# Moving the statistics and scaling of the gated branch into the gate pairs of a fused encoder layer

## The chip, the cores and the metric

The kernel runs on one core of one Trainium2 chip. The metric is the device time of one execution, in microseconds (us). The core's engines each run their own instruction stream in order and meet at semaphores: TensorE (PE, matrix products), VectorE (DVE, element-wise work and statistics), ScalarE (ACT, activations and copies), GpSimd (POOL, here a few element-wise operations and two short reciprocal-root steps) and SyncE (SP, which issues most of the loads).

## The reference

One layer of an encoder on x of 512 tokens by 1024 features, all in float32. The part around the change is the spatial gating branch (SGU):

```python
h = _rmsnorm(x, g_pre_mix)
proj = h @ w_in
q, k, v, g, u, sv, a_ret, a_sgu = jnp.split(proj, list(np.cumsum(IN_SPLITS)[:-1]), axis=-1)
y_ret = _retention_branch(q, k, v, g, ret_decay_logit, w_ret_o)
y_sgu = _sgu_branch(u, sv, sgu_ln_g, sgu_ln_b, w_spatial, b_spatial, w_sgu_o)
merged = jax.nn.sigmoid(a_ret) * y_ret + jax.nn.sigmoid(a_sgu) * y_sgu
x = x + _rmsnorm(merged @ w_out, g_post_mix)
...
def _sgu_branch(u, sv, sgu_ln_g, sgu_ln_b, w_spatial, b_spatial, w_sgu_o):
    u = jax.nn.gelu(u)
    sv = _layernorm(jax.nn.gelu(sv), sgu_ln_g, sgu_ln_b)
    svc = sv.reshape(B, S // CHUNK, CHUNK, SGU_GROUPS, SGU_GW)
    mixed = jnp.einsum('gpq,bnqgc->bnpgc', w_spatial, svc) + b_spatial.T[None, None, :, :, None]
    y = u * mixed.reshape(B, S, SGU_W)
    return y @ w_sgu_o
```

After it a second residual block follows: an RMS norm, an up projection to 2 x 2816, a convolution over three tokens, a gate and a down projection. The retention branch is a chunkwise recurrence over four heads, of which only the layer-normalized, gated result matters here: it is the input of w_ret_o.

## The kernel before

Products are taken in float32 accuracy from float32r halves: each weight block is split into a high part, which ACT copies (L95), and a low part, which DVE subtracts (L112), and three products are summed. Many products of the input with w_in run as a two-by-two Strassen (Winograd) scheme of seven smaller products; the weight forms it needs (T1 to T4, differences and sums of the weight blocks) are made on DVE or POOL (L194, L195, L197, L200) ahead of their splits. Raw weights come in by loads of 512 KB that SP issues (L165 for an ordinary block, L187 and L188 for the two halves of a Strassen pair) into four buffers named raw; a load is issued when the last split that reads the buffer's old content is done.

The stages follow each other on PE: q and k; the retention heads; v, g and sv; four *u pairs*; four *gate pairs* for a_ret, each with two column blocks of w_ret_o; four gate pairs for a_sgu, each with two column blocks of w_sgu_o, which read y; W_out; the feed-forward block.

A pair (class `Pair`) makes two 128-column strips of u or of a gate for all 512 tokens by seven products of twelve 256-column matmuls (L901): `part1` has the product with the first half of x (copied from its bank to c0 by ACT), `second` (the other half, added to c0 by DVE, L922), S1 and S2 (S2 goes on in the bank that ACT copied from, and is copied to c1). `part2` has S3, whose copy DVE subtracts from S1's bank (L940). `part3` has the last two: one goes on in the first bank, and S4 goes on in S1's bank, so S4 waits for L940. Then DVE scales (L949, L954) and ACT applies the function (L950, L955). In the first u pair, S1 and S2 are written ahead of `second`. In a gate pair of a_ret, `f_block` (eight rows of three 512-column matmuls, L286 to L288) stands before `part2`, and a second `f_block` has `part3` in its middle.

`sv_group` makes sv: its products, the finishing additions on DVE (L762), gelu on ACT (L756), a bn_stats on DVE (L757) behind each of the eight gelus, four bn_aggr (L785), and a reciprocal root on POOL (L445, L448). `sv_norm` (L793, eight instructions) subtracts the mean and scales; it is written behind `part2` of the first u pair. `mix(j)` is the spatial mixing of one 128-column strip j of eight: eight matmuls (L984) on sv, and on DVE an addition of the bias (L978), a scale (L992), the product with u (L1000) and the split of y. mix(2j) and mix(2j+1) are written behind gate pair j.

A scheduler orders the written instructions for each engine; `tc.issue_after(i)` adds that what is written inside it comes behind instruction i. Within an engine the order is then fixed.

Of the kernel before, what the change touches and what calls it, by code (L numbers as in the profile page):

```python
# [10 lines left out]
F32 = mybir.dt.float32  # L11
F32R = mybir.dt.float32r
AF = mybir.ActivationFunctionType
ALU = mybir.AluOpType
# [33 lines left out]
def tile_block(ctx: ExitStack, tc, xT, x, wall, par, cs, wsp, bsp, gpost, gffn, out):  # L48
# [11 lines left out]
    def blk(dt=F32, n="blk", shape=(P, S)):  # L60
        return sb.tile(list(shape), dt, tag="blk", bufs=NBLK, name=nm(n))
# [9 lines left out]
    def hi192(n, dt=F32R):  # L71
        pad("hi192")
        return sb.tile([P, S], dt, tag="hi192", bufs=5, name=nm(n))

    def lo64(n, dt=F32R):
        pad("lo64")
        return sb.tile([P, S], dt, tag="lo64", bufs=5, name=nm(n))
# [19 lines left out]
    def two(t):  # L97
        return t.rearrange("p (n c) -> p n c", n=2)
# [21 lines left out]
    i = 0  # L120
    while i < NW:
        pair = [(f, i) for f in FORMS]
        if i == SV0:
# [3 lines left out]
            i = U0  # L127
# [6 lines left out]
        elif i == UP0 + 2 * COUPLES[0][0]:  # L134
# [3 lines left out]
            i = UP0 + 2 * COUPLES[-1][1] + 2  # L138
# [10 lines left out]
    v = nc.vector  # L149
# [144 lines left out]
    T0, T1 = slice(0, 256), slice(256, 512)  # L294
# [156 lines left out]
    for t in range(NT):  # L451
        for n in range(2):
# [3 lines left out]
                out=xt, in_=xt, func=AF.Square, accum_out=ss[:, 4 * n + t : 4 * n + t + 1]  # L456
# [19 lines left out]
    for c in range(19, 1, -2):  # L476
        v.scalar_tensor_tensor(
            out=lc, in0=lc, scalar=1.0 / c, in1=lb, op0=ALU.add, op1=ALU.mult
        )
    v.scalar_tensor_tensor(out=lc, in0=lc, scalar=1.0, in1=la, op0=ALU.add, op1=ALU.mult)  # L480
    with behind():
        v.tensor_scalar(out=lg, in0=lgt, scalar1=0.0, scalar2=None, op0=ALU.min)
    v.scalar_tensor_tensor(
        out=lg, in0=lc, scalar=-2.0, in1=lg, op0=ALU.mult, op1=ALU.add
# [5 lines left out]
    for m in range(8):  # L490
        t = blk(n="qkraw")
# [6 lines left out]
    for m in range(8):  # L498
        t = blk(n="swap")
# [33 lines left out]
    for i, op in enumerate((ALU.max, ALU.min)):  # L533
        v.tensor_scalar(
            out=near[:, i * P : (i + 1) * P], in0=dist[:, P : 2 * P], scalar1=0.0, scalar2=None, op0=op
# [182 lines left out]
    svz = {}  # L718
    sst = const("sst", [P, NT, 2, 6])
    smv = const("smv", [P, NT, 2])  # L720
    srstd = const("srstd", [P, NT])

    def sv_group():

        held = {}

        def product(bank, act, first, last):
            for kp in range(2):
                wh, wl = w_get()
                for t in range(2):  # L730
                    c = slice(t * P, (t + 1) * P)
                    for kk in range(2):
                        k, f = 2 * kp + kk, slice(kk * S, (kk + 1) * S)
                        ah, al = act(k)
                        for i, (a_, w_) in enumerate(((ah, wh), (ah, wl), (al, wh))):
                            nc.tensor.matmul(
                                bank[t], a_[:, c], turns(w_[:, f]), start=first and k == i == 0,
                                stop=last and k == 3 and i == 2, skip_group_check=True,
                            )
                yield  # L740

        def x_(k0, t):
            return lambda k: (xh[k0 + k][:, t], xl[k0 + k][:, t])

        def s_(n):
            return lambda k: forms[n][k]

        def save(n, bank, t0, nh):
            held[n] = [blk(n="sv") for _ in range(2)]
            for t in range(2):  # L750
                svz[t0 + t, nh] = held[n][t]
                copy(held[n][t], bank[t])

        def gelu(t, nh, src):
            z = svz[t, nh]
            nc.scalar.activation(out=z, in_=src, func=AF.Gelu_apprx_tanh, scale=rstd[:, t : t + 1])  # L756
            v.bn_stats(out=sst[:, t, nh, :], in_=z)  # L757

        def finish(n, bank, t0, nh, sub):
            for t in range(2):  # L760
                a, b = (bank[t], held[n][t]) if sub != "held" else (held[n][t], bank[t])
                (v.tensor_sub if sub else v.tensor_add)(held[n][t], a, b)  # L762
                gelu(t0 + t, nh, held[n][t])

        b0 = [ps(), ps()]
        yield from product(b0, x_(0, T0), True, False)
        save("M1", b0, 0, 0)
        b2 = [ps(), ps()]
        yield from product(b2, s_("S1"), True, False)
        save("M5", b2, 2, 1)  # L770
        yield from product(b0, s_("S2"), False, False)
        save("U2", b0, 0, 1)
        for _ in zip(product(b2, s_("S4"), False, True), product(b0, s_("S3"), False, False)):
            yield
        finish("U2", b2, 0, 1, "bank")
        finish("M5", b0, 2, 1, "held")
        b1 = [ps(), ps()]
        yield from product(b1, x_(4, T0), True, True)
        finish("M1", b1, 0, 0, "")
        yield from product(b0, x_(4, T1), False, True)  # L780
        for t in range(2):
            svz[2 + t, 0] = blk(n="sv")
            gelu(2 + t, 0, b0[t])
        for t in range(NT):
            v.bn_aggr(out=smv[:, t, :], in_=sst[:, t].rearrange("p a b -> p (a b)"))  # L785
        rsqrt(srstd, smv[:, :, 1], 1.0, NT)
        yield

    def sv_norm():
        for t in range(NT):  # L790
            for q in range(2):
                z = svz[t, q]
                v.tensor_scalar(  # L793
                    out=z, in0=z, scalar1=smv[:, t, 0:1], scalar2=srstd[:, t : t + 1],
                    op0=ALU.subtract, op1=ALU.mult,
                )


    ogh, ogl = [], []
# [73 lines left out]
    def f_block(ah, al, n, between=None):  # L873

        wh, wl = w_get()
        o = ps()
        for k in range(n):
            if between and k == n // 2:
                between()
            c = slice(k * P, (k + 1) * P)  # L880
            mm3(o, wh[:, c], wl[:, c], turns(ah[k]), turns(al[k]), k == 0, k == n - 1)
        return o

    class Pair:
# [31 lines left out]
        def part1(self, apart=False):  # L916

            c0, c1 = self.t

            def second():  # L920
                o = self.product(1, self.x(4, T0), True)
                v.tensor_add(two(c0[:, T0]), o, two(c0[:, T0]))  # L922

            o = self.product(0, self.x(0, T0), True)
            copy(two(c0[:, T0]), o)
            if not apart:
                second()
            self.product(2, self.s("S1"), True)
            o = self.product(0, self.s("S2"), False)
            copy(two(c1[:, T0]), o)  # L930
            if apart:
                second()
            if self.scale is not None:
                v.tensor_mul(c0[:, T0], c0[:, T0], self.scale[:, T0])
# [27 lines left out]
    for j in range(KD // 2):  # L962
        p = Pair(AF.Gelu_apprx_tanh, lambda: U_HOMES.pop()(), None, rbc)
        with tc.issue_after(summed) if j == 0 else ExitStack():
            p.part1(j == 0)
        if late:
            late.part3()
        p.part2()
        late = p
        uT += p.t  # L970
        if j == 0:
            sv_norm()
    yh, yl = [], []

    def mix(j):
        gs = slice((j // 2) * P, (j // 2 + 1) * P)
        add = tmp("add", (P, P))
        v.scalar_tensor_tensor(  # L978
            out=add, in0=rws[:, gs], scalar=col(LNB + j), in1=bst[:, gs],
            op0=ALU.mult, op1=ALU.add,  # L980
        )
        o = ps()
        for t in range(NT):
            nc.tensor.matmul(  # L984
                o[:, t * P : (t + 1) * P],
                svz[t, j // 4][:, (j % 4) * P : (j % 4 + 1) * P],
                wst[:, gs],
                start=True,
                stop=True,
            )  # L990
        m = tmp("mix")
        v.scalar_tensor_tensor(  # L992
            out=m.rearrange("p (t q) -> p t q", t=NT),
            in0=o.rearrange("p (t q) -> p t q", t=NT),
            scalar=col(LNG + j),
            in1=add[:, None, :].to_broadcast([P, NT, P]),
            op0=ALU.mult,
            op1=ALU.add,
        )
        v.tensor_mul(uT[j], m, uT[j])  # L1000
        h_, l_ = blk(F32R, "yh"), blk(F32R, "yl")
        split(h_, l_, uT[j])
        yh.append(h_)
        yl.append(l_)


    def gated_pair(ah, al, late=None):

        p = Pair(AF.Sigmoid, lambda: tmp("sig"), None, rbc)
        with tc.issue_after(late.last.ins) if late else ExitStack():  # L1010
            p.part1()
        if late:
            with tc.issue_after(p.last.ins):
                late.part3()
        o = [f_block(ah, al, KD)]
        p.part2()
        o.append(f_block(ah, al, KD, p.part3))
        return zip(o, p.t)

    r = []  # L1020
    for j in range(KD // 2):
        for o, t in gated_pair(ogh, ogl, late if j == 0 else None):
            b = (lo64("r", F32) if j == 0 else hi192("r", F32) if j < 3 else blk(n="r"))
            v.tensor_mul(two(b), in_turn(o), two(t))
            r.append(b)
        mix(2 * j)
        mix(2 * j + 1)
    mh, ml = [], []
    for j in range(KD // 2):
        for i, (o, t) in enumerate(gated_pair(yh, yl)):  # L1030
# [589 lines left out]
```

## Time and profile before

| | us |
|---|---|
| median of 3 runs | 794.61 (794.57 to 794.67) |
| profiled execution | 795.35 |
| its span, first to last instruction | 793.5 |
| PE busy | 778.5 (98%) |
| DVE busy | 647.9 (82%) |
| ACT busy | 460.7 (58%) |
| POOL busy | 90.7 (11%) |

The mean granted clock of PE is 0.994. Rows of a timeline give the start in the span, the duration (a matmul's includes its way through the array, so durations overlap), the engine, the line and operation, what it writes and reads, and in brackets how long the engine stood idle before it and what ended that. "x4" means four such instructions in a row. Where a row stands for several, its time is theirs together.

### The profile page before, as it was taken

The numbers are of one execution on the slowest core, as the hardware profiler recorded it, in microseconds if no ns is written. First come the engines' busy times: TensorE is split into PE (matmuls) and PEld (weight loads), VectorE is DVE, ScalarE is ACT, GpSimd is POOL, SyncE is SP. The second block draws the span as 40 slices with busy tenths as digits, with TensorE's granted clock in tenths as the row PEclk, the third lists the DMA queues.
The fourth block names the chain that finished last, engine by engine and source line by source line (L and its number), as shares of the span: only waits on it lengthen the run. The fifth ranks groups of instructions, "written<-read, shape, count | busy, mean of one in ns | idle before, by whom it ended". The sixth has DMA issues, their size and how long they took to land.

```text
span 793.5 us, 13415 instructions
## 1 busy us (share of the span) xinstructions
PE 778.5 (98%) x5139; PEld 723.2 (91%) x5139; DVE 647.9 (82%) x1118; ACT 460.7 (58%) x840; POOL 90.7 (11%) x105
## 2 busy tenths in 40 slices
PE   9999999999899999999999999999999999999996
PEld 8888998988798999999998898999999998999996
DVE  7469987989997877777766659999999889876887
ACT  6546557675655544444445677667777578744442
POOL 0010010010003011132210210001111012200001
PEclk9999999999899999999999999999999999999999
DMA  8755224112233322323349111335555365733244
GB/s 290 270 147 187 80 81 159 53 58 89 80 107 134 106 100 87 107 97 110 109 169 339 67 55 67 114 113 139 139 141 147 114 182 123 169 113 108 101 165 159
DMA packets 35535, 102.68 MB, mean 129 GB/s; under 512 B 4304, under 2 KB 6224, under 8 KB 35472
## 3 DMA queue, kind: packets, MB, share of 16 engines
q1 hardware_dynamic: 29216, 89.91, 33.6%
q0 software_dynamic: 5392, 10.75, 6.4%
q10 hardware_dynamic: 864, 1.18, 0.4%
q8 instruction: 40, 0.66, 0.3%
q14 instruction: 23, 0.19, 0.1%
HBM read 89.24 MB, written 4.19 MB: 118 GB/s over the span
## 4 chain that ended last, share of the span: by engine, by line
PE 63%; DVE 16%; DMA 7%; ACT 6%; issue 5%; POOL 1%; SPq 1%; POOLq 0%; DVEq 0%; ACTq 0%
PE ps L901 22%; PE ps L287 9%; PE ps L286 9%; PE ps L288 9%; DMA raw<-wall 4%; PE ps L1314 3%; PE ps L629 2%; PE ps L630 2%; PE ps L628 2%; DVE dl L112 2%; DVE sl L112 1%; PE ps L1064 1%; PE ps L1063 1%; PE ps L1062 1%; ACT wh L95 1%
## 5 line engine op out<-in xcount | busy, mean ns | idle before, releaser
L112 DVE TENSOR_TENSOR wl<-raw,wh 128x1024 fp32r<-128x1024 f32 (+1 forms) x84 | 95.8, 1150 | 46.6 <-PE ps L901 15.7
L95 ACT ACTIVATE wf<-raw 128x512 fp32r<-128x512 f32 x140 | 83.9, 624 | 79.7 <-PE ps L287 29.2
L901 PE MATMUL ps<-sh,wf 128*128 128x256 f32 x640 | 118.7, 278 | 5.1 <-ACT u L95 3.5
L112 DVE TENSOR_TENSOR wf<-raw,wf 128x512 fp32r<-128x512 f32 x140 | 101.4, 739 | 15.2 <-ACT wf L95 14.9
L901 PEld LDWEIGHTS ps<-sh,wf 128*128 128x128 f32 x640 | 103.2, 194 | 6.0 <-ACT u L95 3.6
L95 ACT ACTIVATE wh<-raw 128x1024 fp32r<-128x1024 f32 (+2 forms) x88 | 84.7, 974 | 31.9 <-DMA raw<-wall 15.3
L287 PE MATMUL ps<-h2l,wh 128*128 128x512 f32 (+1 forms) x256 | 90.2, 354 | 0.3 <-DVE h2l L1135 0.3
L288 PE MATMUL ps<-h2h,wl 128*128 128x512 f32 (+1 forms) x256 | 90.1, 353 | 0.0
L286 PE MATMUL ps<-h2h,wh 128*128 128x512 f32 (+1 forms) x256 | 90.1, 354 | 0.0
L901 PE MATMUL ps<-sl,wf 128*128 128x256 f32 x320 | 88.7, 277 | 0.0
L901 PEld LDWEIGHTS ps<-sl,wf 128*128 128x128 f32 x320 | 62.1, 194 | 0.4
L1314 PE MATMUL ps<-dl,fh 128*128 128x256 f32 x216 | 59.7, 276 | 0.3 <-DVE dl L112 0.3
L1314 PE MATMUL ps<-dh,fh 128*128 128x256 f32 x216 | 59.5, 275 | 0.0
L1314 PE MATMUL ps<-dh,fl 128*128 128x256 f32 x216 | 59.4, 275 | 0.0
L95 ACT ACTIVATE dh<-raw 128x768 fp32r<-128x768 f32 (+1 forms) x36 | 33.6, 949 | 36.2 <-DVE raw L220 21.4
L901 PE MATMUL ps<-xh,wf 128*128 128x256 f32 x288 | 53.7, 279 | 0.0
L288 PEld LDWEIGHTS ps<-h2h,wl 128*128 128x128 f32 x256 | 48.5, 190 | 5.1
L287 PEld LDWEIGHTS ps<-h2l,wh 128*128 128x128 f32 x256 | 48.6, 190 | 5.0 <-DVE h2l L1135 0.5
L286 PEld LDWEIGHTS ps<-h2h,wh 128*128 128x128 f32 x256 | 48.4, 190 | 4.8 <-ACT h2h L1132 0.3
L630 PE MATMUL ps<-wh,xl 128*128 128x512 f32 x128 | 48.5, 379 | 0.0
L629 PE MATMUL ps<-wl,xh 128*128 128x512 f32 x128 | 48.5, 379 | 0.0
L628 PE MATMUL ps<-wh,xh 128*128 128x512 f32 x128 | 48.5, 380 | 0.0
(335 smaller groups left out, 2147.9 us busy)
## 6 DMA issues: line engine op xcount, KB each, us to landing
raw<-wall SPq DMA_DIRECT2D x144, 512.0 KB, 3.6
x<-x SPq DMA_DIRECT2D x24, 256.0 KB, 5.7
fl<-gp POOLq DMA_DIRECT2D x12, 256.0 KB, 3.8
swap<-qkraw SPq DMA_DIRECT2D x16, 128.0 KB, 2.3
x<-x POOLq DMA_DIRECT2D x8, 256.0 KB, 2.4
fl<-fs POOLq DMA_DIRECT2D x8, 256.0 KB, 4.0
xT<-xT SPq DMA_DIRECT2D x7, 256.0 KB, 5.2
xT<-xT POOLq DMA_DIRECT2D x4, 256.0 KB, 4.0
```

The lines of the kernel that those rows point to most:

```text
L95: return nc.scalar.activation(out=o, in_=i, func=AF.Copy)
L112: nc.vector.tensor_sub(lo, src, as32(hi))
L286: nc.tensor.matmul(o, ah, bh, start=start, stop=False, skip_group_check=skip)
L287: nc.tensor.matmul(o, ah, bl, start=False, stop=False, skip_group_check=skip)
L288: nc.tensor.matmul(o, al, bh, start=False, stop=stop, skip_group_check=skip)
L628: nc.tensor.matmul(acc[t], xh[k][:, c], turns(wh[:, f]), start=k == 0, stop=False)
L629: nc.tensor.matmul(acc[t], xh[k][:, c], turns(wl[:, f]), start=False, stop=False)
L630: part_end[0] = nc.tensor.matmul(acc[t], xl[k][:, c], turns(wh[:, f]), start=False, stop=k == KD - 1)
L901: self.last = nc.tensor.matmul(o, w_[:, c], a_, start=first and k == n == 0, stop=k == 3 and n == 2, skip_group_check=True,)
L1062: nc.tensor.matmul(o, ah, turns(bh), start=k == 0, stop=False)
L1063: nc.tensor.matmul(o, ah, turns(bl), start=False, stop=False)
L1314: nc.tensor.matmul(o, a_[:, c], turns(w_[:, f]), start=j == t == i == 0, stop=j == DP - 1 and i == 2 and n not in (M2, M3, M4), skip_group ...
```

## The change

The bn_stats leave the gelus of sv's stage. A new function, `sv_stats`, holds all eight, the four bn_aggr, the reciprocal root and the first half of the scaling, `sv_norm(0)`; it is written in gate pair 0 behind `part2`, and nothing of it comes ahead of the addition of that pair's `second` (`p.sum`). `sv_norm(q)` now scales one half of the columns, four instructions; `sv_norm(1)` is written at the same place of gate pair 1. The first gate pair has no mixing behind it, the second has mix(0) and mix(1), the third three, the fourth three. The homes of the tiles r change so that the strips of sv and u that live longer have theirs. No instruction is added or removed on any engine. Lines shift in the changed kernel: L757 is now L788, L762 L761, L785 L789, L793 L796, L901 L904, L922 L925, L940 L943, L949 L952, L954 L957.

```diff
--- before.py
+++ after.py
@@ -754,7 +754,6 @@
         def gelu(t, nh, src):
             z = svz[t, nh]
             nc.scalar.activation(out=z, in_=src, func=AF.Gelu_apprx_tanh, scale=rstd[:, t : t + 1])
-            v.bn_stats(out=sst[:, t, nh, :], in_=z)
 
         def finish(n, bank, t0, nh, sub):
             for t in range(2):
@@ -781,19 +780,23 @@
         for t in range(2):
             svz[2 + t, 0] = blk(n="sv")
             gelu(2 + t, 0, b0[t])
+        yield
+
+    def sv_stats():
         for t in range(NT):
+            for nh in range(2):
+                v.bn_stats(out=sst[:, t, nh, :], in_=svz[t, nh])
             v.bn_aggr(out=smv[:, t, :], in_=sst[:, t].rearrange("p a b -> p (a b)"))
         rsqrt(srstd, smv[:, :, 1], 1.0, NT)
-        yield
-
-    def sv_norm():
+        sv_norm(0)
+
+    def sv_norm(q):
         for t in range(NT):
-            for q in range(2):
-                z = svz[t, q]
-                v.tensor_scalar(
-                    out=z, in0=z, scalar1=smv[:, t, 0:1], scalar2=srstd[:, t : t + 1],
-                    op0=ALU.subtract, op1=ALU.mult,
-                )
+            z = svz[t, q]
+            v.tensor_scalar(
+                out=z, in0=z, scalar1=smv[:, t, 0:1], scalar2=srstd[:, t : t + 1],
+                op0=ALU.subtract, op1=ALU.mult,
+            )
 
 
     ogh, ogl = [], []
@@ -919,7 +922,7 @@
 
             def second():
                 o = self.product(1, self.x(4, T0), True)
-                v.tensor_add(two(c0[:, T0]), o, two(c0[:, T0]))
+                self.sum = v.tensor_add(two(c0[:, T0]), o, two(c0[:, T0])).ins
 
             o = self.product(0, self.x(0, T0), True)
             copy(two(c0[:, T0]), o)
@@ -968,8 +971,6 @@
         p.part2()
         late = p
         uT += p.t
-        if j == 0:
-            sv_norm()
     yh, yl = [], []
 
     def mix(j):
@@ -1004,7 +1005,7 @@
         yl.append(l_)
 
 
-    def gated_pair(ah, al, late=None):
+    def gated_pair(ah, al, late=None, extra=None):
 
         p = Pair(AF.Sigmoid, lambda: tmp("sig"), None, rbc)
         with tc.issue_after(late.last.ins) if late else ExitStack():
@@ -1014,17 +1015,20 @@
                 late.part3()
         o = [f_block(ah, al, KD)]
         p.part2()
+        if extra:
+            with tc.issue_after(p.sum):
+                extra()
         o.append(f_block(ah, al, KD, p.part3))
         return zip(o, p.t)
 
     r = []
     for j in range(KD // 2):
-        for o, t in gated_pair(ogh, ogl, late if j == 0 else None):
-            b = (lo64("r", F32) if j == 0 else hi192("r", F32) if j < 3 else blk(n="r"))
+        for o, t in gated_pair(ogh, ogl, late if j == 0 else None, {0: sv_stats, 1: lambda: sv_norm(1)}.get(j)):
+            b = (lo64("r", F32) if j == 0 else blk(n="r") if j == 1 else hi192("r", F32))
             v.tensor_mul(two(b), in_turn(o), two(t))
             r.append(b)
-        mix(2 * j)
-        mix(2 * j + 1)
+        for i in ((), (0, 1), (2, 3, 4), (5, 6, 7))[j]:
+            mix(i)
     mh, ml = [], []
     for j in range(KD // 2):
         for i, (o, t) in enumerate(gated_pair(yh, yl)):
```

The scheduler's order moves in three places. On ACT, at the first u pair, these rows stand before; `sv` are the gelus, `rws` a row sum of the spatial weights, `wf` splits of weights, and the two `u` are the copies of the first bank (S2 waits for the first):

```order
L756 ACTIVATE sv_1794<-sv_1794,rstd 128x512
L756 ACTIVATE sv_1795<-sv_1795,rstd 128x512
L756 ACTIVATE sv_2206<-ps_1731,rstd 128x512
L756 ACTIVATE sv_2209<-ps_1732,rstd 128x512
L95 ACTIVATE rws_1909<-ps_2219 128x512
L95 ACTIVATE wf_2169<-raw_2104 128x512
L95 ACTIVATE wf_2184<-raw_2098 128x512
L95 ACTIVATE wf_2191<-raw_2187 128x512
L95 ACTIVATE wf_2230<-raw_2188 128x512
L95 ACTIVATE u_2225<-ps_2227 128x256
L95 ACTIVATE u_2226<-ps_2227 128x256
```

and these now:

```order
L756 ACTIVATE sv_1794<-sv_1794,rstd 128x512
L95 ACTIVATE wf_2159<-raw_2093 128x512
L756 ACTIVATE sv_1795<-sv_1795,rstd 128x512
L95 ACTIVATE wf_2163<-raw_2100 128x512
L95 ACTIVATE wf_2178<-raw_2094 128x512
L756 ACTIVATE sv_2200<-ps_1731,rstd 128x512
L95 ACTIVATE wf_2185<-raw_2181 128x512
L756 ACTIVATE sv_2202<-ps_1732,rstd 128x512
L95 ACTIVATE rws_1909<-ps_2204 128x512
L95 ACTIVATE wf_2215<-raw_2182 128x512
L95 ACTIVATE u_2210<-ps_2212 128x256
```

The first gelu pair no longer stand together, three weight splits stand between the gelus, and the split of the newest load (`wf_2230`, now `wf_2215`) still stands just ahead of the first copy; between the copies there are now splits. On PE, three of the twelve matmuls of `second` stood between S1 and S2 of this u pair before; now the twelve of each product stand together, p0, S1, S2, `second`.

On DVE, in the same stretch, the statistics stand between the finishing additions and the splits before:

```order
L762 TENSOR_TENSOR sv_1794<-ps_2095,sv_1794 128x512
L762 TENSOR_TENSOR sv_1795<-ps_2096,sv_1795 128x512
L112 TENSOR_TENSOR wf_2165<-raw_2097,wf_2165 128x512
L757 BN_STATS sst<-sv_1794 128x6
L757 BN_STATS sst<-sv_1795 128x6
L200 TENSOR_TENSOR raw_2104<-raw_2104,raw_2098 128x512
L757 BN_STATS sst<-sv_2206 128x6
L757 BN_STATS sst<-sv_2209 128x6
L112 TENSOR_TENSOR wf_2169<-raw_2104,wf_2169 128x512
L112 TENSOR_TENSOR wf_2184<-raw_2098,wf_2184 128x512
L112 TENSOR_TENSOR wf_2191<-raw_2187,wf_2191 128x512
```

and now:

```order
L761 TENSOR_TENSOR sv_1794<-ps_2091,sv_1794 128x512
L200 TENSOR_TENSOR raw_2100<-raw_2100,raw_2094 128x512
L112 TENSOR_TENSOR wf_2140<-raw_2094,wf_2140 128x512
L761 TENSOR_TENSOR sv_1795<-ps_2092,sv_1795 128x512
L112 TENSOR_TENSOR wf_2159<-raw_2093,wf_2159 128x512
L112 TENSOR_TENSOR wf_2163<-raw_2100,wf_2163 128x512
L112 TENSOR_TENSOR wf_2178<-raw_2094,wf_2178 128x512
L194 TENSOR_TENSOR raw_2231<-raw_2181 128x512
L112 TENSOR_TENSOR wf_2185<-raw_2181,wf_2185 128x512
```

The bn_stats are gone, and the addition L200 and a split of `raw_2094` stand between the two finishing additions, ahead of the split of `raw_2093`; the latter was `raw_2097` before, and its buffer takes the next load.

On DVE in gate pair 0, before, behind the additions of the u pair before it; L940 with `sig_2721<-ps_2724` is the difference for which S4 of this gate pair waits:

```order
L112 TENSOR_TENSOR wl_2757<-raw_2754,wh_2756 128x1024
L194 TENSOR_TENSOR raw_2825<-raw_2772 128x512
L949 TENSOR_TENSOR u_2594<-ps_2596,rbc_574 128x256
L112 TENSOR_TENSOR wf_2776<-raw_2772,wf_2776 128x512
L195 TENSOR_TENSOR raw_2772<-raw_2772,raw_2773 128x512
L952 TENSOR_TENSOR u_2595<-ps_2598,u_2595 128x256
L112 TENSOR_TENSOR wf_2822<-raw_2773,wf_2822 128x512
L954 TENSOR_TENSOR u_2595<-u_2595,rbc_574 128x512
L978 SCALAR_TENSOR_TENSOR add_2945<-rws_1909,part,bst_2223 128x128
L112 TENSOR_TENSOR wf_2829<-raw_2825,wf_2829 128x512
L112 TENSOR_TENSOR wf_2857<-raw_2825,wf_2857 128x512
L940 TENSOR_TENSOR sig_2721<-ps_2724,sig_2721 128x256
```

and now, from the second bn_aggr on:

```order
L789 BN_AGGR smv<-sst 128x2
L788 BN_STATS sst<-sv_1910 128x6
L788 BN_STATS sst<-sv_2202 128x6
L789 BN_AGGR smv<-sst 128x2
L788 BN_STATS sst<-sv_1911 128x6
L789 BN_AGGR smv<-sst 128x2
L112 TENSOR_TENSOR wf_2806<-raw_2802,wf_2806 128x512
L112 TENSOR_TENSOR wf_2834<-raw_2802,wf_2834 128x512
L796 TENSOR_SCALAR sv_1794<-sv_1794,smv,srstd 128x512
L943 TENSOR_TENSOR sig_2698<-ps_2701,sig_2698 128x256
L796 TENSOR_SCALAR sv_1795<-sv_1795,smv,srstd 128x512
L796 TENSOR_SCALAR sv_2200<-sv_2200,smv,srstd 128x512
```

Ahead of that difference, now L943 with `sig_2698<-ps_2701`, stand all eight bn_stats, four bn_aggr and the first of the norms, which waits for POOL; three more norms stand behind it.

## The prediction

> **What bounds the kernel now.** The page's busy line (us, share of the span, instructions) is read first: TensorE (PE) is the bound.
>
> ```profile
> PE 778.5 (98%) x5139; PEld 723.2 (91%) x5139; DVE 647.9 (82%) x1118; ACT 460.7 (58%) x840; POOL 90.7 (11%) x105
> ```
>
> So only what makes PE idle, or slows its clock, can change the time. PE's waits (second view: waited-for line, us in total, times, longest) name two that matter, one of 3.5 us and one of 1.6 us.
>
> ```profile
> PE ps L901 <- ACT u L95: 3.5, 1, 3.5
> PE ps L901 <- ACT sig L95: 1.6, 1, 1.6
> PE ps L388 <- PEq L1610: 0.8, 1, 0.8
> ```
>
> The third view, PE's timeline, places them. The first row is the last matmul of S1 before `second` of the first u pair; the third is its S2 product, waiting for ACT's copy of the first u bank; the fourth is S2 of gate pair 0.
>
> ```profile
> 203.85 0.28 PE L901 MATMUL ps<-sh,wf 128*128 128x256 f32 x1
> 203.97 0.28 PE L901 MATMUL ps<-xh,wf 128*128 128x256 f32 x1
> ...
> 204.19 0.28 PE L901 MATMUL ps<-xh,wf 128*128 128x256 f32 x1
> 207.92 0.58 PE L901 MATMUL ps<-sh,wf 128*128 128x256 f32 x1 [3.46 <-ACT u L95]
> ...
> 248.22 0.38 PE L901 MATMUL ps<-sh,wf 128*128 128x256 f32 x1 [1.65 <-ACT sig L95]
> ```
>
> Matmuls start 0.11 us apart, so the first stall delays issue by 207.92 - 204.30 = 3.62 us, the second by 1.65 + 0.28 - 0.11 = 1.82 us. The first costs more than its length. The stretches (length, PE, PEld, DVE, ACT, POOL busy, granted clock, DMA share, GB/s), cut where the clock can step:
>
> ```profile
> 203.32:206.73 3.41, 1.14 (x11) 0.95 (x9) 3.41 (x7) 3.40 (x7) 0.00 (x0) 0.96 0.46 154
> 206.73:210.15 3.42, 2.23 (x10) 2.23 (x11) 2.90 (x9) 1.03 (x3) 1.49 (x2) 0.50 0.43 149
> 210.15:213.56 3.41, 3.41 (x19) 3.41 (x18) 2.99 (x6) 2.05 (x4) 0.38 (x1) 0.54 0.04 10
> 244.28:247.69 3.41, 2.30 (x21) 2.10 (x19) 3.41 (x7) 2.39 (x6) 1.27 (x1) 1.00 0.02 4
> 220.00:240.00 20.00, 20.00 (x181) 20.00 (x181) 20.00 (x40) 12.80 (x26) 0.72 (x1) 1.00 0.30 98
> ```
>
> A stretch with PE 33% busy (1.14 of 3.41) is followed by two at half clock; one with 67% (2.30 of 3.41) is not. From 207.92 to 213.56 PE did at half clock what full clock does in about half of it: 5.64 x 0.48 = 2.7 us lost. The two stalls together cost 3.62 + 2.7 + 1.82 = 8.1 us.
>
> Why the first wait ends so late is read from the chain of waits (start, us, what) and from DVE's and ACT's timelines.
>
> ```profile
> 202.76 0.61 DVE wf L112
> ...
> 203.39 3.49 DMA raw<-wall
> ...
> 206.97 0.63 ACT wf L95
> 207.60 0.28 ACT u L95
> ...
> 207.92 14.09 PE ps L901 x101
> ```
>
> ```profile
> 191.32 0.68 DVE L757 BATCH_NORM_STATS2 sst<-sv 128x6 f32<-128x512 f32 x1
> ...
> 197.89 0.68 DVE L757 BATCH_NORM_STATS2 sst<-sv 128x6 f32<-128x512 f32 x1
> ...
> 203.28 1.28 DVE L757 BATCH_NORM_STATS2 sst<-sv 128x6 f32<-128x512 f32 x2
> 204.48 0.67 DVE L200 TENSOR_TENSOR raw<-raw,raw 128x512 f32<-128x512 f32 x1
> ...
> 208.06 0.42 DVE L785 BATCH_NORM_AGGREGATE smv<-sst 128x2 f32<-128x12 f32 x4
> ...
> 210.57 0.55 DVE L793 TENSOR_SCALAR sv<-sv,smv,srstd 128x512 f32<-128x512 f32 x1 [0.93 <-POOL srstd L448]
> ...
> 218.55 2.83 DVE L793 TENSOR_SCALAR sv<-sv,smv,srstd 128x512 f32<-128x512 f32 x6
> ```
>
> ```profile
> 202.20 1.33 ACT L756 ACTIVATE sv<-sv,rstd 128x512 f32<-128x512 f32 x2 [1.99 <-DVE sv L762]
> 203.44 1.25 ACT L756 ACTIVATE sv<-ps,rstd 128x512 f32<-128x512 f32 x2
> 204.58 0.59 ACT L95 ACTIVATE rws<-ps 128x512 f32<-128x512 f32 x1
> 205.19 2.41 ACT L95 ACTIVATE wf<-raw 128x512 fp32r<-128x512 f32 x4
> ```
>
> DVE, busy without a break, splits a weight form late (202.76); only that frees the raw buffer for the next load (203.39, landed 206.88); ACT has the split of that load queued ahead of the u copy. DVE's pitch is 0.60 us for a 512-column operation (two bn_stats in 1.28, the next row 1.20 later), 0.47 for a norm (six in 2.83), 0.34 for 256 columns, 0.10 for a bn_aggr.
>
> **The change, part by part.** *The first stall.* Eight bn_stats leave sv's stage. Four of them (191.32 to 197.89) stood ahead of the split at 202.76; the L200 addition, behind it before, now stands ahead of it. The split moves from 202.76 to 202.76 - 4 x 0.60 + 0.60 = 200.96, the load's issue to 201.6, its landing (3.49 later) to 205.1. ACT is then free too: from about 201.0 the order gives it three gelus (0.62 each, from the rows above), rws and three splits (0.55 each), to 205.1. Its split of the load (0.63) and the copy (0.28) end at 206.0; PE starts S2 at 206.1. Its S1 ends at 203.97 as before, and `second` now stands behind S2, so PE idles 2.15 us where it idled 3.62.
>
> *The clock behind it.* In 203.32 to 206.73 PE would be busy 0.81 us (to 204.13) and 0.61 (from 206.1): 42%, between the 33% that lowered the clock and the 67% that didn't. It is nearer to 33%, so I take a drop to half; but the next stretch would be full of matmuls, so only one is cold, 3.41 x 0.48 = 1.64 us instead of 2.7. Ends: 0 and 2.7. [...]
>
> *The second stall.* The wait for the sig copy is a queue behind DVE:
>
> ```profile
> 243.38 0.69 DVE L112 TENSOR_TENSOR wf<-raw,wf 128x512 fp32r<-128x512 f32 x1 [1.50 <-ACT wf L95]
> ...
> 246.56 0.68 DVE L954 TENSOR_TENSOR u<-u,rbc 128x512 f32<-128x512 f32 x1
> 247.16 0.41 DVE L940 TENSOR_TENSOR u<-ps,u 128x256 f32<-128x256 f32 x1
> ```
>
> ```profile
> 247.27 0.63 ACT L955 ACTIVATE u<-u 128x512 f32<-128x512 f32 x1 [0.54 <-DVE u L954]
> 247.81 0.37 ACT L95 ACTIVATE sig<-ps 128x256 f32<-128x256 f32 x1
> ```
>
> Between 190 and this place DVE loses 8 x 0.60 + 0.42 + 8 x 0.47 + 0.93 (the wait for POOL) = 9.9 us, while PE comes 2.5 to 4.2 us earlier. Walked with these pitches, DVE's L954 ends at P + 0.9 (P: start of gate pair 0 on PE, 242.39 before, about 239.8 after), the sig copy at P + 2.6; S2 needs it at P + 4.0. The stall goes: 1.82 us. Its cover is 1.4 us.
>
> *The new wait in gate pair 0.* Now DVE does there 8 bn_stats, 4 bn_aggr, the POOL round trip and a norm, all ahead of the difference (L943 after, L940 before) that frees the bank for PE's S4 product at P + 18.4. Before, that difference ran right behind the splits. What starts the sequence is a pair of loads:
>
> ```profile
> 238.57 8.42 SPq L165 DMA_DIRECT2D raw<-wall  x2
> 248.20 0.33 SPq L187 DMA_DIRECT2D raw<-wall  x1
> 248.80 0.33 SPq L188 DMA_DIRECT2D raw<-wall  x1
> ```
>
> ```profile
> 254.54 0.69 DVE L194 TENSOR_TENSOR raw<-raw 128x512 f32<-128x512 f32 x1 [2.00 <-DMA raw<-wall]
> ```
>
> By the walk they go out at P + 1.9 and P + 2.9. Loads take 3.5 us alone (203.39) but 6.3 us where three follow closely (248.20 to 254.54). After the landing DVE needs: L194 0.60, a 1024-column split 1.13, L195 0.60, L952 and L955 0.67, two splits and L957 1.8, six bn_stats 3.6, aggregates 0.4, POOL's trip 2.1 (from the end of the aggregates at 208.48 to the norm at 210.57; it hides two splits), the norm 0.47, L943 0.34: 11.7 us. So L943 ends at P + 1.9 + 6.3 + 11.7 = P + 19.9, and S4 waits 1.6 us; with 3.5 us it ends 1.3 us early and nothing waits. The order again sends three loads close together, so I take 1.6; ends 0 and 1.6.
>
> *The rest.* sv_norm(1) is four norms (1.9 us) in gate pair 1, where by the same walk S4's difference has about 3 us to spare. Six of the eight mixes move one pair later.
>
> ```profile
> L984 PE MATMUL ps<-wst,sv x64: 273/275/275, 266.7 to 333.0; 128*128 128x128 f32 x64
> ```
>
> Each is eight matmuls, about 0.9 us that PE spends either way, and on DVE three 512-column and one 128-column operation, about 2.1 us; what stands behind them on DVE is the second f_block's split, needed some 8 us later. Three mixes now end the last gate pair instead of two; the products that read y reach its last rows over 2.5 us after they are written. Cost nothing; that cover gone, the third mix would show as up to 2.1 us. POOL's two rsqrt rows move behind one L197, the r tiles' homes cost nothing, and SP's queue keeps its order.
>
> *Sum.* Before 8.1; after 2.15 + 1.64 + 1.6 = 5.4: 2.7 us faster. Against the profiled execution (795.35 us, span 793.5 and 1.85 around it; 0.74 above the median) that is 792.6; against the median 794.61 it is 791.9.
>
> **The rivals.** *No clock drop* (42% busy is enough): 2.15 + 1.6 = 3.75 left, 790.2; without the new wait 788.6. For it: no row shows how much a stretch must hold. Against it: 42% is nearer the row that dropped. [...]
>
> *About the same: the first load is slow.* If the load of 201.6 takes 6.3 us like those of 248.20, it lands at 207.9, PE starts at 208.9: 4.9 us idle, then 213.56 - 208.9 = 4.7 us cold, 2.2 lost; with 1.6 that is 8.7 against 8.1, 795.2. For it: DMA share was 0.46 there. Against it: the same load took 3.49 in the same place.
>
> *Slower: DVE is still behind when the statistics come.* DVE is busy 20.00 of 20.00 us from 220 to 240. If it reaches gate pair 0 as late against PE as before (L940 at P + 4.8, by my walk P + 1.3), everything behind shifts 3.5 us: S4 waits 5.1 us, long enough for a cold clock (two stretches, about 2.5), and the sig wait stays (1.8): 2.15 + 1.64 + 5.1 + 2.5 + 1.8 = 13.2, 5.1 us slower, 799.7. It decides from about 2.5 us behind my walk, where the S4 wait passes 4 us and brings a cold stretch. Against it: 9.9 us of work are gone and DVE idled 1.50 us at 243.38 even before.
>
> **Chances.** 0.2% is 1.6 us, about what a measurement of this kernel tells from no change. Forecast (one cold stretch) 0.42, its own range 790.2 to 793.2 (the new wait 0 to 1.6, and 1.3 for the walk's error); no drop 0.26; about the same 0.15; slower 0.17. Faster 0.68, same 0.15, slower 0.17. From 788.6 (no drop, no new wait) to 795.6 all but the slower case and a small tail lie inside.
>
> **What would show it.** Right: the u wait about 2 us, one half-clock stretch from 206.73, no sig wait, a PE wait of up to 1.6 us on DVE L943 near 258, no PE wait at the start of the second gates. Wrong: a u wait of 3 us or more, no or two cold stretches, or an S4 wait above 3 us with a cold stretch behind it.

## The result

The changed kernel takes 794.66 us (median of 20 runs, 792.79 to 797.39), the kernel before 794.69 us (20 runs, 793.33 to 797.09). The ratio is 1.0001, with a 95% interval of 0.9991 to 1.0011: the change moves the time by nothing that can be measured. The profiled execution of the changed kernel has a span of 794.4 us, the one of before 793.5.

Under that equal sum much has moved. PE's waits in the profile after (line waited for, us in total, times, longest):

```profile
PE ps L904 <- DVE sig L943: 3.3, 1, 3.3
PE ps L904 <- ACT u L95: 2.6, 2, 1.9
PE ps L388 <- PEq L1614: 0.8, 1, 0.8
```

And where they stand in PE's timeline: the first u pair, the last u pair (233.47) and S4 of gate pair 0 (261.09). Ahead of the two long waits stands the last matmul before them.

```profile
203.58 0.28 PE L904 MATMUL ps<-sh,wf 128*128 128x256 f32 x1
205.76 0.38 PE L904 MATMUL ps<-sh,wf 128*128 128x256 f32 x1 [1.91 <-ACT u L95]
...
233.47 0.38 PE L904 MATMUL ps<-sh,wf 128*128 128x256 f32 x1 [0.64 <-ACT u L95]
...
257.54 0.28 PE L904 MATMUL ps<-xh,wf 128*128 128x256 f32 x1
261.09 0.58 PE L904 MATMUL ps<-sh,wf 128*128 128x256 f32 x1 [3.27 <-DVE sig L943]
```

The first wait has shrunk, the wait for the sig copy is gone, and a wait for L943 has come. The stretches of the changed kernel's profile (length, PE, PEld, DVE, ACT, POOL busy, granted clock, DMA share, GB/s), cut where its clock steps:

```profile
201.82:205.24 3.42, 2.04 (x19) 1.84 (x17) 2.92 (x5) 3.26 (x7) 0.00 (x0) 1.00 0.71 216
205.24:208.65 3.41, 2.88 (x25) 2.89 (x26) 3.38 (x7) 2.53 (x6) 0.00 (x0) 1.00 0.26 96
256.44:259.85 3.41, 1.37 (x13) 1.18 (x11) 2.44 (x5) 0.00 (x0) 2.56 (x3) 1.00 0.00 0
259.85:263.26 3.41, 2.17 (x10) 2.18 (x11) 3.41 (x6) 0.00 (x0) 0.56 (x1) 0.50 0.00 0
263.26:266.68 3.42, 3.42 (x11) 2.88 (x11) 2.32 (x5) 2.54 (x4) 0.00 (x0) 0.50 0.48 153
```

In these two profiles the half-clock time has not gone: it has moved from behind the first u wait to behind the wait for L943, and there it is as long (two stretches) as it was before.

Taking the same matmul (by its number among the 5139) in the two traces, the changed kernel's start minus that of before is a running account (from 270 to 335 us PE's order differs between the two, so no row is taken there):

| place | after minus before, us | step |
|---|---|---|
| ahead of the first u wait | -0.3 | |
| behind it and behind the half clock of before | -4.4 | 4.1 won: a shorter wait, no half clock |
| behind the wait at 233 | -3.5 | 0.9 lost |
| behind the sig copy's place | -5.2 | 1.7 won |
| S4 of gate pair 0 starts | -1.7 | 3.4 lost: the wait for L943 |
| behind the half clock there | +1.1 | 2.8 lost |
| first products of the second half (515) | +0.9 | |
| last matmul | +0.6 | |

So 5.8 us were won, and 7.1 lost, of it 6.2 at one place. From there on the two run side by side; nothing is paid for the later mixing. This is an account of one execution of each kernel, and these two differ by 0.9 us where the medians don't differ.

Before, the difference came at 261.48 and PE at 262.80, so S4 didn't wait:

```profile
261.48 0.42 DVE L940 TENSOR_TENSOR sig<-ps,sig 128x256 f32<-128x256 f32 x1
```

```profile
262.80 0.28 PE L901 MATMUL ps<-sh,wf 128*128 128x256 f32 x1
```

Now PE is there at 257.65. Why L943 comes only at 260.62, in the changed kernel's DVE timeline:

```profile
241.49 0.41 DVE L943 TENSOR_TENSOR u<-ps,u 128x256 f32<-128x256 f32 x1
...
247.11 0.69 DVE L194 TENSOR_TENSOR raw<-raw 128x512 f32<-128x512 f32 x1 [1.16 <-DMA raw<-wall]
247.72 1.22 DVE L112 TENSOR_TENSOR wl<-raw,wh 128x1024 fp32r<-128x1024 f32 x1
248.85 1.77 DVE L195 TENSOR_TENSOR raw<-raw,raw 128x512 f32<-128x512 f32 x1
250.54 0.41 DVE L952 TENSOR_TENSOR u<-ps,rbc 128x256 f32<-128x256 f32 x1
...
256.91 0.21 DVE L789 BATCH_NORM_AGGREGATE smv<-sst 128x2 f32<-128x12 f32 x1
257.04 1.24 DVE L112 TENSOR_TENSOR wf<-raw,wf 128x512 fp32r<-128x512 f32 x2
259.21 1.49 DVE L796 TENSOR_SCALAR sv<-sv,smv,srstd 128x512 f32<-128x512 f32 x1 [0.93 <-POOL srstd L448]
260.62 0.41 DVE L943 TENSOR_TENSOR sig<-ps,sig 128x256 f32<-128x256 f32 x1
```

and in its POOL timeline:

```profile
248.69 1.38 POOL L197 TENSOR_TENSOR raw<-raw,raw 128x512 f32<-128x512 f32 x1 [8.81 <-DMA raw<-wall]
257.21 0.52 POOL L445 TENSOR_SCALAR rs<-smv 128x4 f32<-128x4 f32 x1 [7.14 <-DVE smv L789]
257.81 1.36 POOL L448 TENSOR_TENSOR srstd<-rs,nhalf 128x4 f32<-128x4 f32 x1
259.16 1.25 POOL L200 TENSOR_TENSOR raw<-raw,raw 128x512 f32<-128x512 f32 x1
```

From the landing (247.11) to the end of L943 (261.03) DVE takes 13.9 us, where the prediction had 11.7. The difference is in two rows: L195 occupies DVE 1.69 us to the next row instead of 0.60, and the norm 1.41 instead of 0.47. Both begin inside an addition of POOL (248.69 to 250.07, 259.16 to 260.41), and they end 0.55 and 0.29 us after it.

### The profile page after: what moved, and what is told of

Same layout as the page of the kernel before. It is cut to its first block, busy times and chain, and to the rows that moved or that the text cites. A ratio compares the mean times of both kernels' runs of the same rounds, so it can differ in the third digit from the quotient of the medians.

```text
span 794.4 us, 13407 instructions
## 1 busy us (share of the span) xinstructions
PE 778.2 (98%) x5139; PEld 723.0 (91%) x5139; DVE 652.3 (82%) x1118; ACT 461.5 (58%) x840; POOL 86.9 (11%) x105
## 4 chain that ended last, share of the span: by engine, by line
PE 78%; DVE 13%; DMA 3%; issue 2%; ACT 2%; POOL 1%; POOLq 0%; DVEq 0%; SPq 0%; ACTq 0%
PE ps L904 18%; PE ps L286 11%; PE ps L287 11%; PE ps L288 11%; PE ps L1318 10%; PE ps L628 3%; PE ps L629 3%; PE ps L630 3%; DMA raw<-wall 3%; DVE wf L112 2%; DVE sl L112 2%; PE ps L1334 2%; PE ps L1068 1%; PE ps L1067 1%; PE ps L1066 1%
## 5 line engine op out<-in xcount | busy, mean ns | idle before, releaser
L904 PE MATMUL ps<-sh,wf 128*128 128x256 f32 x640 | 118.7, 278 | 5.8 <-DVE sig L943 3.3
L904 PEld LDWEIGHTS ps<-sh,wf 128*128 128x128 f32 x640 | 102.8, 194 | 7.0 <-DVE sig L943 3.5
L904 PE MATMUL ps<-sl,wf 128*128 128x256 f32 x320 | 88.6, 277 | 0.0
L904 PEld LDWEIGHTS ps<-sl,wf 128*128 128x128 f32 x320 | 62.0, 194 | 0.4
L904 PE MATMUL ps<-xh,wf 128*128 128x256 f32 x288 | 52.5, 276 | 0.0
```

The source lines that it names most:

```text
L904: self.last = nc.tensor.matmul(o, w_[:, c], a_, start=first and k == n == 0, stop=k == 3 and n == 2, skip_group_check=True,)
```

## The experiments

**Statistics behind L943** (e1_behind_diff). One edge moved:

```diff
-            v.tensor_sub(two(c1[:, T1]), self.two(self.b[2][:, T0]), two(c1[:, T1]))
+            self.diff = v.tensor_sub(two(c1[:, T1]), self.two(self.b[2][:, T0]), two(c1[:, T1])).ins
...
-            with tc.issue_after(p.sum):
+            with tc.issue_after(p.diff):
                 extra()
```

> The changed kernel with one edge moved: statistics and norms come behind the subtraction (L943) that S4 waits for, instead of behind the addition of `second`. Theory (the first stall's gain was real, and was eaten in gate pair 0 by a 3.4 us wait of S4 and the 2.8 us of half clock behind it): S4 of gate pair 0 doesn't wait, no half-clock stretch there, and the kernel is about 5 to 6 us faster than before (789 to 790, ratio 0.993). Rival (DVE is simply late in gate pair 0, whatever stands ahead of L943): S4 still waits 2 us or more and the ratio stays within 0.997 to 1.003.

Measured: 791.43 us, ratio 0.9956 (0.9942 to 0.9971), 0.4% faster. S4 doesn't wait: in this kernel's DVE timeline L943 stands at 254.53, ahead of all statistics.

```profile
254.53 0.42 DVE L943 TENSOR_TENSOR sig<-ps,sig 128x256 f32<-128x256 f32 x1
254.86 1.87 DVE L788 BATCH_NORM_STATS2 sst<-sv 128x6 f32<-128x512 f32 x3
```

Beside these three bn_stats POOL adds:

```profile
254.69 1.28 POOL L200 TENSOR_TENSOR raw<-raw,raw 128x512 f32<-128x512 f32 x1 [5.14 <-DVE wf L112]
```

The gain at the first stall was real, and the wait for L943 was what ate it. It is smaller than the 5 to 6 us expected, and one reason is seen: behind the first wait this profile has a half-clock stretch that the changed kernel's has not. Its stretches:

```profile
202.75:206.16 3.41, 1.43 (x13) 1.24 (x12) 3.03 (x6) 3.19 (x7) 0.00 (x0) 1.00 0.70 234
206.16:209.57 3.41, 3.41 (x18) 3.41 (x17) 2.68 (x5) 1.14 (x3) 0.00 (x0) 0.50 0.03 8
```

**Norms a gate pair later** (e2_norm_later). The bn_stats stay ahead of L943; POOL's trip and the norm no longer do.

```diff
         rsqrt(srstd, smv[:, :, 1], 1.0, NT)
-        sv_norm(0)
...
-{0: sv_stats, 1: lambda: sv_norm(1)}
+{0: sv_stats, 1: lambda: sv_norm(0), 2: lambda: sv_norm(1)}
```

> The changed kernel with only the norms one gate pair later (first half in gate pair 1, second half in gate pair 2); the eight bn_stats stay ahead of L943 in gate pair 0. Theory (the trip to POOL and the norm behind it, 3.7 us from the last bn_aggr to L943 less two splits of 1.2, are what pushed the wait past a clock window): S4 waits 0 to 1 us, no half-clock stretch, 4 to 5 us faster than before (790, ratio 0.994 to 0.995). Rival (the bn_stats themselves are too much there): S4 waits 2 us or more, ratio 0.997 or above.

Measured: 791.21 us, ratio 0.9943 (0.9927 to 0.9959), 0.6% faster. L943 (L942 here) comes right behind the two splits at 258.34 and PE waits 1.0 us, without a half-clock stretch (mean granted clock of this profile 0.998):

```profile
258.82 0.38 PE L903 MATMUL ps<-sh,wf 128*128 128x256 f32 x1 [1.01 <-DVE sig L942]
```

S4 starts 1.2 us late here (1.0 us idle) instead of 3.4. So the eight bn_stats ahead of L943, with L195 still held up by POOL (1.76 us), cost 1.2 us there, and the trip to POOL with one norm behind it 2.3 us and the 2.8 us of half clock: 5 of the 6.2 us lost.

**The first part alone** (e4_stats_in_u). Statistics and all norms in the first u pair, the mixing as before.

```diff
         uT += p.t
+        if j == 0:
+            with tc.issue_after(p.sum):
+                sv_stats()
+                sv_norm(1)
```

> Only the first part of the change: the bn_stats leave sv's stage, but statistics and all eight norms come in the first u pair behind the addition of its `second`; mixing as before the change. Theory (DVE is the limit over the u pairs, so time won at the first stall is waited for again at gate pair 0): the first u wait is about 2 us without a cold stretch (4 us won), and PE then waits 4 us or more in u pairs and gate pair 0 together; ratio 0.997 to 1.003. Rival (the place of the statistics doesn't matter once they are out of sv's stage): ratio 0.995.

Measured: 795.07 us, ratio 1.0000 (0.9988 to 1.0012). The first wait is 2.2 us; a second of 2.2 us comes in the third u pair, for a weight split that DVE reaches late behind the statistics and the eight norms. Each has a half-clock stretch in this profile (mean granted clock 0.994).

```profile
227.01 0.49 PE L904 MATMUL ps<-sh,wf 128*128 128x256 f32 x2 [2.21 <-DVE wf L112]
```

```profile
203.78:207.19 3.41, 1.20 (x11) 1.01 (x10) 3.02 (x6) 3.17 (x7) 0.00 (x0) 1.00 0.68 235
224.26:227.67 3.41, 1.20 (x10) 1.01 (x10) 3.41 (x7) 1.15 (x2) 0.00 (x0) 1.00 0.00 0
```

The ratio is the theory's, the way to it is not. The theory had no half-clock stretch at the first wait; with it PE is only 2.0 us ahead of the kernel before behind that wait. The second wait and its stretch cost 3.75 us, in the u pairs; S4 of gate pair 0 doesn't wait. At this place in the u pairs the statistics win nothing; other places there weren't run.

**The mixing alone** (e5_mix_later): the kernel before with none, two, three and three mixes behind the four gate pairs and the homes of r that go with it.

```diff
-        mix(2 * j)
-        mix(2 * j + 1)
+        for i in ((), (0, 1), (2, 3, 4), (5, 6, 7))[j]:
+            mix(i)
```

> The kernel before with only the mixing moved (none, two, three, three behind the four gate pairs) and the homes of r that go with it. Theory (the mixing's place costs and brings nothing): the same stalls as before, ratio 0.999 to 1.001. Rival (the three mixes at the end delay the products on y, or the mixes of gate pair 0 were in the way): a new PE wait of 0.5 us or more near the first products on y, or the time moves by 1 us or more.

Measured: 795.54 us, ratio 1.0000 (0.9988 to 1.0012): the mixing's place costs nothing that can be measured. PE waits nowhere near the first products on y. The profiled execution, 799.32 us, was the longest of its eleven. It has a wait of 2.4 us near 47 us, far from the change, where the other profiles have 0.8 us at most; and its wait for the sig copy is 2.4 us, not 1.6, with a half-clock stretch behind it (mean granted clock 0.992, where the profile of before has 0.994). Why the sig wait is longer in this execution is not known.

**POOL's additions on DVE** (e6_adds_dve), for the first two gate pairs, with L943 of gate pair 0 held behind the first norm as in the changed kernel.

```diff
-            eng = nc.vector if i < GATE0 or i >= UP0 else nc.gpsimd
+            eng = nc.vector if i < GATE0 + 8 or i >= UP0 else nc.gpsimd
...
+            with tc.issue_after(normed[n]):
+                d = p.diff()
```

> The changed kernel with POOL's weight additions (L197, L200) of the first two gate pairs on DVE, and L943 of gate pair 0 held behind the first norm, as it stands in the changed kernel. Theory (DVE is held up while POOL adds: the L195 of 1.77 us and the norm of 1.49 us in the changed kernel overlap POOL's two additions): L195 takes 0.68 us, the first norm 0.55 us, no DVE row above 0.7 us for 512 columns there; from the landing to L943 about 13.7 us (13.9 - 1.1 - 0.95 for the two rows, + 0.6 for the addition, + 1.2 for two splits that no longer hide POOL's trip), S4 waits about 3.1 us, time within 0.3% of before. Rival (these rows are long for another reason, the loads or the order): they stay at 1.5 to 1.8 us and S4 waits about 5.2 us.

Measured: 793.58 us, ratio 0.9978 (0.9966 to 0.9990). Its DVE timeline:

```profile
245.86 0.69 DVE L194 TENSOR_TENSOR raw<-raw 128x512 f32<-128x512 f32 x1 [0.93 <-DMA raw<-wall]
...
247.61 0.69 DVE L195 TENSOR_TENSOR raw<-raw,raw 128x512 f32<-128x512 f32 x1
...
258.27 0.55 DVE L798 TENSOR_SCALAR sv<-sv,smv,srstd 128x512 f32<-128x512 f32 x1 [1.21 <-POOL srstd L448]
258.73 0.42 DVE L951 TENSOR_TENSOR sig<-ps,sig 128x256 f32<-128x256 f32 x1
```

With none of POOL's additions there, L195 takes 0.69 us and the norm 0.55, as expected; from the landing to the end of the difference it is 13.3 us, with two operations more on DVE. S4 waits 2.4 us (expected 3.1, by the rival 5.2), with one half-clock stretch (mean granted clock 0.996). The time is 0.2% below before. The two rows were long because of POOL.

**The copy ahead of the late split** (e8_copy_first): statistics behind L943, and in the first u pair the split of the late load held behind ACT's copy of the bank.

```diff
-        while w_pos[1] < len(units) and (w_pos[1] <= i or
+        while w_pos[1] < len(units) and (u_copied or units[w_pos[1]] != ("B21", U0 + 2)) and (w_pos[1] <= i or
...
-            w_ready[w_pos[1]] = w_unit(u)
+            with tc.issue_after(u_copied[0]) if u == ("B21", U0 + 2) else ExitStack():
+                w_ready[w_pos[1]] = w_unit(u)
...
-            copy(two(c0[:, T0]), o)
+            u_copied.append(copy(two(c0[:, T0]), o).ins)
```

> Statistics behind L943 as in e1_behind_diff, and in the first u pair ACT's copy of the bank comes ahead of the split of the late load. Theory (the first wait is that one split; a gap with under about 1.95 us of idle time in a 3.41 us stretch never lowers the clock): the first wait falls from 2.0 to about 1.4 us and no profile shows a half-clock stretch; about 0.9 us of it is waited for later in the u pairs, so the median is 789.7 to 790.8 (ratio 0.9935 to 0.995) and the runs lie closer together than those of e1_behind_diff. Rival (PE then waits for the same load elsewhere, or the u pairs on DVE take all of it): ratio 0.9955 to 0.997.

Measured: 789.50 us, ratio 0.9928 (0.9914 to 0.9942), 5.7 us faster than before and the lowest median here. The first gap between matmul starts is 1.38 us where it was 2.2, PE waits again at 231.75 to 232.73, and the stretch with the first wait keeps its clock:

```profile
203.14:206.56 3.42, 2.31 (x21) 2.12 (x20) 3.08 (x6) 3.15 (x7) 0.00 (x0) 1.00 0.73 248
```

Its six runs lie within 2.9 us (788.14 to 791.00), the nine of e1_behind_diff within 4.2. Whether it is faster than e1_behind_diff is not shown: the two intervals meet at 0.9942, and the two further runs of that kernel, taken beside this one (789.79 and 790.61, below), lie inside its six. One profile without a half-clock stretch doesn't show that none ever has one, either.

**The kernel of e1_behind_diff twice more**, for its clock.

> The kernel of e1_behind_diff again, for its clock. Theory (the clock falls behind a stretch of 3.41 us that is less than some 43% busy, and the stretches lie at random against the program): the same first wait of 2.0 us, with a half-clock stretch behind it in about half of the executions; where it is missing, PE waits about 0.9 us later in the u pairs. Rival (the kernel's own timing decides): a half-clock stretch of 3.41 us behind the first wait as in the first profile.

> As e1_again_a: with theory one or the other, depending on where the stretch begins; with the rival always the half-clock stretch.

Measured: 789.79 and 790.61 us, one execution each. The first wait is 2.1 us in both. The first execution, where the stretch's border falls into the wait, keeps the clock:

```profile
201.40:204.81 3.41, 2.75 (x25) 2.56 (x23) 2.70 (x5) 3.41 (x7) 0.00 (x0) 1.00 0.49 159
204.81:208.22 3.41, 1.99 (x17) 1.99 (x18) 3.11 (x6) 2.72 (x7) 0.00 (x0) 1.00 0.47 154
```

The second, where the wait lies inside one stretch, loses it:

```profile
203.45:206.87 3.42, 1.37 (x12) 1.18 (x11) 3.04 (x6) 3.19 (x7) 0.00 (x0) 1.00 0.75 247
206.87:210.28 3.41, 3.41 (x18) 3.41 (x18) 2.81 (x5) 1.26 (x3) 0.00 (x0) 0.50 0.05 17
```

The same program with the same wait pays a half-clock stretch or doesn't, by where the stretches happen to begin. How often it does, three profiles can't tell. The other half of the expectation failed: where the clock is kept, PE does not wait 0.9 us later in the u pairs.

## Why the prediction was right and wrong

The forecast of 791.9 us, with its own range of 790.2 to 793.2, was missed: the time is 794.66. The outer range, 788.6 to 795.6, holds it, and "same" had a chance of 0.15, but neither for the reason that came. Both stalls shrank as forecast; a wait of S4 twice as long as forecast, half-clock time behind it that the sum had at nothing, and a wait of 0.9 us that it hadn't at all took the gain back. That the two come out equal is luck. Of the prediction's own signs of being wrong, two came: no half-clock stretch behind the u wait, and an S4 wait above 3 us with half clock behind it.

*The first stall: right.* It forecast the split at 200.96, the load's issue at 201.6 and its landing at 205.1, and 2.15 us of idle; the trace has 200.61, 201.32, 204.73 and 2.07 us (205.76 less 203.58 and one pitch of 0.11). The order and the pitches of before were enough. From the chain of waits:

```profile
200.61 0.69 DVE wf L112
...
201.32 3.40 DMA raw<-wall
```

(In the prediction's rows of PE it is the fourth, not the third, that is the first u pair's S2, and the fifth that is gate pair 0's.)

*The clock behind the first stall: wrong in the step that laid the stretches.* The prediction took the borders of the one profile (203.32, 206.73) as fixed and asked whether 42% is enough there. The borders lay elsewhere in the other executions: in the changed kernel's profile one falls at 205.24, inside the wait, and the two stretches are 60% and 84% busy, so no clock was lost there. The prediction's border was off even for the kernel before: its clock steps at 206.45, not at 206.73, and ended there the stretch that lowered it reads 42%, where the prediction read 33%:

```profile
203.04:206.45 3.41, 1.42 (x13) 1.23 (x12) 3.41 (x7) 3.40 (x7) 0.00 (x0) 1.00 0.46 154
```

So 42% is not between the two cases, it is the very case that lowered the clock: in the runs above 1.37 and 1.43 of 3.41 us (40% and 42%) lowered it as well, wherever a stretch was left that empty. For the kernel of e1_behind_diff "one cold stretch" and "no cold stretch" were thus two phases of the same program, and for such a wait the term is a mean over both. For the changed kernel itself it stays open whether any phase costs clock: its wait, 1.91 us idle, would leave 44% if it lay whole in one stretch, and the runs show only that 42% lost the clock (1.98 us idle, e1_behind_diff) and 45% kept it (1.87 us, e2_norm_later).

*The second stall: right.* It is gone, with 1.7 us.

*The new wait in gate pair 0: the mechanism right, its size wrong.* It forecast 1.6 us at S4 (its own terms, P + 19.9 less P + 18.4, give 1.5), on L943, and at 258; it is 3.4 us at 257.65. Gate pair 0 starts at P = 238.94. The loads went out later than walked, from P + 3.6 on and not P + 1.9, and DVE began 4.6 us after the first of them, not 6.3: at P + 8.2, as walked, because the two errors cancel.

```profile
242.53 0.33 SPq L187 DMA_DIRECT2D raw<-wall  x1
```

The step that failed is the term for DVE's sequence: it took 13.9 us instead of 11.7, and 2.0 of the 2.2 us are L195 and the norm under POOL's additions. The trace of before did show the effect, in a 1024-column split of 1.64 us (1.22 at 263.05, with POOL idle) that begins inside POOL's L200, and the working didn't ask why that row was long. Its DVE and POOL rows:

```profile
244.99 1.64 DVE L112 TENSOR_TENSOR wl<-raw,wh 128x1024 fp32r<-128x1024 f32 x1
```

```profile
239.28 3.41 POOL L197 TENSOR_TENSOR raw<-raw,raw 128x512 f32<-128x512 f32 x1 [28.74 <-ACT wf L95]
244.16 1.39 POOL L200 TENSOR_TENSOR raw<-raw,raw 128x512 f32<-128x512 f32 x1 [1.47 <-DVE wf L112]
```

Not every row of DVE is long beside POOL. L195 (1.77 us), the norm (1.49) and that split (1.64) are. Three bn_stats took 1.87 us at 254.86 in the first experiment, beside POOL's L200 from 254.69 to 255.97, and 1.83 at 251.40 in e6_adds_dve with POOL idle; an addition that reads PSUM (L955 at 238.78 in the changed kernel, beside L200 from 238.60) took 0.41, as it does at 251.48 with POOL idle. What sets the two kinds apart, no run shows.

*The clock behind the new wait: missing.* The sum priced the wait at its length alone, and only the slower rival let a wait there lower the clock, from 4 us. At 3.4 us it did, for two stretches: 2.8 us. In e6_adds_dve a wait of 2.4 us did too, for one. With 9.2 us lost at the four places (2.1, 0.9, 3.4, 2.8) against the forecast of 5.4, the gain of 2.7 us became none.

*The rest.* A wait of 0.9 us at 233, where ACT's copy stands behind splits, was not foreseen: PE comes 4 us earlier, and DVE and ACT are not all that much ahead there. That the mixing costs nothing was right. Of the rivals, "slower" had the right place with another cause: DVE was not 3.5 us behind the walk but 1.3 us (L943 of the u strip at 241.49, P + 2.6, walked P + 1.3). "About the same" came true in its sum, not by its slow load, which landed 3.4 us after its issue.

## What to carry to other kernels

Work that is moved out of one stall must be followed to the instruction on the same engine that frees something for the bound engine; one edge that put it behind that instruction instead of ahead of it turned no gain into one of 0.4%. A wait of PE has two prices, its length and the half-clock stretch behind it, and the second is paid in those executions in which the wait leaves one stretch too empty: in the runs here that took between 1.9 and 2.0 us of idle time inside one stretch of 3.41 (1.87 kept the clock, 1.98 lost it). When DVE operations are costed from their usual durations, those that lie beside POOL's additions need their own price (here 1.77 us instead of 0.68 for an addition, 1.49 instead of 0.55 for a norm).

## What the runs showed of the hardware

*The clock's stretches.* Within a profile the steps of the granted clock lie a whole number of 3.41 us apart: at 206.45, 213.28 and 790.13 before (6.83 us, then 576.85, 169 times 3.413) and at 259.85, 266.68 and 788.92 in the changed kernel (6.83, then 522.24, 153 times 3.413). Taken as borders of stretches of that length, they lie elsewhere against the program from execution to execution: in the three profiles of the kernel of e1_behind_diff the stretches around the first wait begin at 202.75, 201.40 and 203.45. Counting PE's busy time in each, as in the rows above and those of before: shares of 0.35 (1.20 of 3.41), 0.40, 0.40, 0.42 and 0.42 were followed by half clock, and so were 0.17, 0.29 and 0.30 in e5_mix_later (waits of 3.3, 2.4 and 2.4 us) and 0.29 in e6_adds_dve (a wait of 2.4); 0.58, 0.60 and 0.68 were not. The nearest on the other side is e2_norm_later, whose first wait leaves 45%, at full clock before and after:

```profile
202.34:205.75 3.41, 1.54 (x15) 1.35 (x13) 3.19 (x6) 3.34 (x8) 0.00 (x0) 1.00 0.83 258
```

At half clock, a stretch 64% busy (2.17 of 3.41, behind S4 of the changed kernel) was followed by another at half clock, one 85% busy (e5_mix_later, from 210.63) and full ones (3.42 of 3.42 from 263.26 in the changed kernel) by full clock. From full clock, 58% of a stretch without work was enough to lower it in these runs (2.0 of 3.41 us, before and in e1_behind_diff).

*DVE beside POOL.* A 512-column addition of DVE (L195) took 0.69 us with POOL idle (e6_adds_dve) and 1.77 us where it began inside POOL's addition of 1.38 us (the changed kernel); a norm 0.55 and 1.49. It was not always DVE's row that was long: in the trace of before POOL's L197 at 239.28, which began while DVE ran one split after the other, took 3.41 us, and DVE's rows kept their 0.68. Beside POOL's small instructions on 128x4 (L445 and L448, 257.21 to 259.17 in the changed kernel) DVE's splits kept their pace: two in 1.24 us at 257.04.

What stays open is how the other nineteen runs of the changed kernel, which have no profile, divide between its stalls' clock phases. The mean granted clock of each run shows that their half-clock time differs: one stretch is 3.41 x 0.5 / 794 = 0.002 of it. The profiled run has 0.992 and took 796.26 us, the three at 0.998 took 793.15 to 793.97. But the five at 0.996 range from 792.79 to 797.17, and half clock behind the last matmul (from 788.92 on in the profiled run) is counted in it as well, so the clock is part of the spread and not all of it.
